# Two changes to a two-layer encoder kernel: some stores issued by ACT, and the last two projection jobs of the second layer taken unit by unit

## The chip, the cores and the metric

The kernel runs on one core of a Trainium2 chip. The time is the device time of one execution in microseconds (us), as the median of several runs. All engines of the core have their own instruction stream: TensorE (PE, with its weight loads shown apart as PEld), VectorE (DVE), ScalarE (ACT), GpSimd (POOL) and SyncE (SP). SP computes nothing here: before the change it issues every DMA of the program.

## The reference

Two groups of tokens go through the same trunk of two layers with the same weights: `x_sample` (1024 tokens, "s" in tile names) and `x_prompt` (512 tokens, "p"). The width is 1024, all in float32. Each layer is

```
h = rmsnorm(x, pre_g) * (1 + scale) + shift        # shift, scale, gate: from c by a matmul
p = h @ w_in                                       # one projection, split into columns
mixed = concat(mixer1(p) * silu(gate1), mixer2(p) * silu(gate2))
x = x + gate * rmsnorm(mixed @ w_out, post_g)
```

Layer 0 mixes with dense attention over 8 query heads that share 2 key heads (mixer A: q and k normalised and rotated), and with a mixture of three dilated sliding windows over 8 heads (mixer B). Layer 1 mixes with attention over a neighbourhood of 8 rows by 16 columns with a learned bias (mixer C, 12 heads), and with a two-dimensional Fourier transform followed by a linear map (mixer D).

## The kernel before

**Units and jobs.** The 1536 tokens are three units of 512: units 0 and 1 are the group s, unit 2 is the group p. A projection is cut into jobs of 256 output columns. In layer 1 the jobs are `u0`, then `k`, `q`, `v` for three blocks of heads (`k0 q0 v0 k1 ...`), and then the gates `g0 g1 g2 d0`. A job loads its weights in four chunks (`load_w`, L375): DMA into a staging tile `ws`, a rounded copy on ACT (tile `wh...`), and the rest of the value on POOL or DVE (`wl...`). A product is then three matmuls: high by high, high by low, low by high. A gate job on one unit is two accumulations of 24 matmuls with 512 columns each (`chan_gemm`; tiles `c1g` for g0 to g2, `c1d` for d0).

**Through memory.** What a projection gives is stored to scratch tensors in HBM and loaded again by the attention. Staging tiles for this are three buffers (tag `sp`, `SPB` = 3). Some are filled by ACT alone: `spill` (L434; tiles `spkb` and `spqb`, k and q of mixer B), and `half_v` (L455; `vstvb`, v of mixer B, and `vst1v`, v of mixer C). The stores to `k0`, `q0`, `vb0` and `v1` follow. Others are filled by ACT and DVE together (`spill_hl`, `spill_gate`).

**The output projection** of a unit needs its operand first (`s3_operand`, L891). For each of eight slices k it loads the mixer's output (`m`) and the gate (`g`) into one of the three `sp` buffers (tile `og`), multiplies them (POOL and DVE in turn, L912), rounds on ACT (`hhm`, L913) and takes the rest on DVE (`hlm`, L914). The products are the tiles `y`, 256 columns a matmul, weights `who` and `wlo`.

**Attention units.** A unit of mixer B is one pair of heads on 512 queries: scores (`sbs`, `sbp`), softmax (DVE, ACT, DVE on the tiles `ebs`, `ebp`), transposes (`pt1bs`, `pt2bs`), copies out of PSUM, and products with v (`obs`, `obp`). In the listings below `obs701` is the product for pair 7 of group s, first half of its queries, second head; `obs410` is pair 4, second half. Mixer C has scores `scs`, transposes `ptcs`, products `ocs` with v tiles `Vcs`.

**The order.** The program names work in the order of `run`. The framework's scheduler (`schedule_with_timeline_sim=True`, L1419) then orders the instructions of each engine by a modelled timeline, so that projection matmuls are put between those of the attention. Each engine runs its list in that order. Every DMA signals on one of eight semaphores, given out in turn, and first waits until the one that had it before has landed. All DMAs are issued at L140.

**The place of the second part.** The end of layer 1's projection goes job by job: in each job unit 0 and then unit 1. In the last job, `d0`, the operand of unit 2's output projection, `s3_operand(1, 2)`, is named between unit 0 and unit 1 (`mid`, L1369). Then follows `s3(1, 2)`, the output projection of unit 2.

Of the kernel before, what the change touches and what calls it, by code (L numbers as in the profile page):

```python
# [122 lines left out]
class Body:  # L123
# [10 lines left out]
        self.read_b = None  # L134


    def dma(self, dst, src):

        dst, src = (t.bitcast(F32) if t.dtype == F32R else t for t in (dst, src))
        self.nc.sync.dma_start(dst, src)  # L140

    def mm(self, out, l, r, start, stop):
        self.nc.tensor.matmul(out, l, r, start=start, stop=stop, skip_group_check=True)  # L143
# [220 lines left out]
    def w_pair(self, shape, name):  # L364
        self.wn += 1
        if self.wend:
            tags, bufs = self.wend[self.wn % len(self.wend)]
            pool = self.wx if tags[0][:2] == "wx" else self.sb
        elif self.wx and self.wn % (WB + WX) >= WB:
            pool, tags, bufs = self.wx, ("wxh", "wxl"), WX  # L370
        else:
            pool, tags, bufs = self.sb, ("wh", "wl"), WB
        return [pool.tile(shape, F32R, tag=t, name=f"w{x}{name}", bufs=bufs) for x, t in zip("hl", tags)]
# [60 lines left out]
    def spill(self, ps, dst, u, scale, nm, classes=False):  # L434

        st = self.sb.tile([P, 2, 512], F32, tag="sp", name="sp" + nm, bufs=SPB)[:, 0]
        self.nc.scalar.mul(st, ps, scale)
        if classes:
            dst, st = (x.rearrange("p (r a) -> p r a", r=4) for x in (dst, st))
            self.dma(dst[:, :, P * u:P * u + P], st)  # L440
        else:
            self.dma(dst[:, u * 512:(u + 1) * 512], st)

    def spill_v(self, ps, nh, dst, nm):

# [99 lines left out]
    def s2_0_unit(self, H, u, w, typ, q, nm):  # L545
        pool = self.l0
        g, gu = self.unit_of[u]
        n = g.name
        if typ in ("ga", "gb"):
            for c in range(2):  # L550
                ps = self.pD(f"g{nm}{c}")
                self.chan_gemm(ps, H, w, c)
                self.flush()
                p = 2 * q + c + (4 if typ == "gb" else 0)
                self.spill_gate(ps, self.gd[0, n, gu, p], f"{nm}{c}")
            return
        toks = []
        for jp in range(2):
            i = 4 * gu + 2 * jp
            ps = self.early.pop((nm, jp), None)  # L560
            if ps is None:
                ps = self.pD(f"t{nm}{jp}").rearrange("p (t c) -> p t c", t=2)
                self.tok_gemm(ps, H, w, jp)
            else:
                self.tok_gemm(ps, H, w, jp, 4)
            if jp == FLUSH:
                self.flush()
            if typ == "vb":
                dst = self.vd[0, n, q].rearrange("(r a) d -> r a d", r=4)[2 * jp:2 * jp + 2, P * gu:P * gu + P]
                self.dma(dst.rearrange("t p d -> p t d"), self.half_v(ps, f"{nm}{jp}"))  # L570
                continue
            js = slice(i, i + 2)
            t = pool.tile([P, 2, 256], F32, tag="qt", name=f"qt{nm}{jp}", bufs=QTB)
            toks.append(t)
            if typ == "kva":
                dst = self.vd[0, n, "a"][i * P:(i + 2) * P].rearrange("(t p) h d -> p t h d", t=2)
                self.spill_v(ps[:, :, 128:256], 2, dst, f"{nm}{jp}")
                self.qk_a(ps[:, :, 0:128], 2, self.tab[:, js], t[:, :, 0:128], f"{nm}{jp}")
            elif typ == "qa":
                self.qk_a(ps, 4, self.tab[:, js], t, f"{nm}{jp}")  # L580
            else:
                self.qk_b(ps, 4, self.tabb[:, js], t, f"{nm}{jp}")
        if typ == "vb":
            return

        def finish():
            for c in range(1 if typ == "kva" else 2):
                pt = (self.pT if self.idle else self.pD)(f"qT{nm}{c}")

                for j in range(4):  # L590
                    o = pt[:, j * P:(j + 1) * P]
                    if typ == "qb":
                        o = pt.rearrange("p (t r a) -> p r t a", t=4, r=4)[:, j]
                    self.tr(o, toks[j // 2][:, j % 2, c * P:(c + 1) * P])
                if typ == "kva":
                    self.spill_hl(pt, self.kd[0, n, 0], gu, 1.0, nm)
                elif typ == "kb":
                    self.spill(pt, self.kd[0, n, 4 + 2 * q + c], gu, 1.0, f"{nm}{c}", g.U > 1)
                elif typ == "qb":
                    self.spill(pt, self.qd[0, n, 4 + 2 * q + c], gu, 0.125, f"{nm}{c}")  # L600
                else:
                    self.spill_hl(pt, self.qd[0, n, 2 * q + c], gu, 0.125, f"{nm}{c}")
        self.late.append(finish)
# [413 lines left out]
        self.Gd = [[dr.tile([P, 2, 256], F32R, name=f"G{x}{cs}") for x in "hl"] for cs in range(2)]  # L1017
        self.bias_dr = dr.tile([16, NCH, 24, 32], F32, name="bias_dr")

    def s2_1_job(self, Hs, us, kind, mid=None):  # L1020
        base = dict(q=0, k=768, v=1536, g=2304, u=3072, d=3328)
        typ, q = kind[0], int(kind[1])
        c0 = base[typ] + 256 * q
        w = self.load_w(self.a["w_in_cd"][0][:, c0:c0 + 256], f"1{kind}{us[0]}", W1)
        for i, u in enumerate(us):
            if i == 1 and mid:
                mid()
            self.s2_1_unit(Hs[u], u, w, typ, q, f"1{kind}{u}")

    def s2_1_unit(self, H, u, w, typ, q, nm):  # L1030
        nc, pool = self.nc, self.sb
# [2 lines left out]
        if typ == "v":  # L1034
            for jp in range(2):
                gr = 2 * gu + jp
                ps = self.pD(f"t{nm}{jp}").rearrange("p (t c) -> p t c", t=2)
                self.tok_gemm(ps, H, w, jp)
                st = self.half_v(ps, f"{nm}{jp}").rearrange("p t (h d) -> p t h d", h=2)
                for t in range(2):  # L1040
                    self.dma(self.vd[1, n, q][:, 2 * t:2 * t + 2, :, gr, :].rearrange("h r c d -> (r c) h d"), st[:, t])
            return
        for c in range(2):
            ps = self.pD(f"c{nm}{c}")
# [205 lines left out]
    def run(self):  # L1250
# [85 lines left out]
        with tc.tile_pool(name="l1", bufs=1) as self.l1:  # L1336
# [26 lines left out]
            for kind, i in zip(jobs[:LEAD], ST2):  # L1363
                step(i[0])
                self.s2_1_job(Hs, [0], kind)
                step(i[1])
            for n, kind in enumerate(jobs):

                mid = (lambda: ops.append(self.s3_operand(1, 2))) if n == len(jobs) - 1 else None  # L1369
                self.s2_1_job(Hs, [1] if kind in jobs[:LEAD] else [0, 1], kind, mid)  # L1370
                if n == 0:
                    second, third = self.fourier(gs)
                if n == FS[0]:
                    four = second()
                if n == FS[1]:
                    third(*four)
                    for q in range(3):
                        self.attn_c(gp, 0, q)
                elif kind[0] == "v":
                    for h in range(2):  # L1380
                        self.attn_c(gs, h, int(kind[1]))
            _, H = self.s3(1, 2, H=ops[0], last=lambda: self.s3_operand(1, 0))
            self.wend = ([(("wh", "wl"), WB)] * WB + [(("wxh", "wxl"), WX)] * WX + [(("qh", "ql"), QB)] * QB +
                         [(("pth", "ptl"), PTB)] * PTB + [(("V", "V"), VB)] * (VB // 2))
# [38 lines left out]
```

## Time and profile before

| | |
|---|---|
| time, median of 3 runs | 1926.3 us (1924.66 to 1928.03) |
| the profiled execution, its own time | 1924.99 us |
| its span, first to last instruction | 1923.1 us |
| PE busy in the span | 1851.2 us, 96% |
| DVE busy | 1204.1 us, 63% |
| ACT busy | 927.0 us, 48% |
| POOL busy | 596.2 us, 31% |
| mean granted clock of PE | 0.986 |

PE is busy nearly all the time, so the reading starts from the 72 us in which it is not, and from the stretches in which its granted clock is 0.5 and not 1. The waits say on whom an engine stood; the timeline of one engine shows single instructions with the idle time before them in square brackets; the windows view gives busy time, granted clock and DMA share of a stretch.

### The profile page before, as it was taken

The page shows a single profiled execution, that of the slowest core. Times are in us where ns is not written, and L with a number is a line of the kernel's source. Part 1 is how long each engine was busy: PE and PEld are TensorE (multiplying, and loading weights), DVE is VectorE, ACT ScalarE, POOL GpSimd, SP SyncE. Part 2 cuts the span into 40 slices and gives each one's busy share as a digit, 9 for nine tenths or more (in the row PEclk, how much of TensorE's full clock was granted, in tenths as well). Part 3 has the DMA queues.
Part 4 walks back from the last instruction along what each step waited for, and adds up shares of the span by engine and source line. Part 5 has one row for each costly group of instructions (what it writes and reads, how often), then busy time and mean ns, then how long its engine had stood idle before and what let it go on. Part 6 is the DMA issues. An engine that isn't in the chain of part 4 may idle for free.

```text
span 1923.1 us, 37887 instructions
## 1 busy us (share of the span) xinstructions
PE 1851.2 (96%) x13752; PEld 1618.0 (84%) x13752; DVE 1204.1 (63%) x3110; ACT 927.0 (48%) x2197; POOL 596.2 (31%) x534
## 2 busy tenths in 40 slices
PE   7999999999999999999999989999999999998998
PEld 5789768999998988889977677888988888887998
DVE  2688863254767666767676687663666666664633
ACT  3456543343356554556554455553544444452421
POOL 3631224354722111121111121443423444322410
PEclk9999999999999999999999999999999999998999
DMA  9754455466663323234345563663777676655743
GB/s 305 252 176 150 125 143 183 124 200 216 230 208 119 104 87 115 69 121 144 118 149 156 163 213 111 219 194 125 224 228 222 201 241 192 205 170 185 234 150 143
DMA packets 255050, 332.51 MB, mean 173 GB/s; under 512 B 25624, under 2 KB 172408, under 8 KB 254864
## 3 DMA queue, kind: packets, MB, share of 16 engines
q1 hardware_dynamic: 254864, 330.10, 54.1%
q8 instruction: 108, 1.77, 0.4%
q14 instruction: 78, 0.64, 0.1%
HBM read 248.42 MB, written 81.61 MB: 172 GB/s over the span
## 4 chain that ended last, share of the span: by engine, by line
PE 41%; DMA 7%; DVE 3%; POOL 1%; issue 1%; ACT 1%; SPq 0%; POOLq 0%; ACTq 0%; DVEq 0%
PE y L143 6%; PE c1g L143 5%; PE c1q L143 5%; PE c1k L143 5%; PE t1v L143 4%; DMA Vcs<-v1s 2%; PE ocs L676 2%; PE ptcs L147 2%; PE scs L143 1%; PE obs L676 1%; PE c1d L143 1%; DMA og<-g1s 1%; PE sbs L807 1%; PE oas L143 1%; DMA og<-g0s 1%
## 5 line engine op out<-in xcount | busy, mean ns | idle before, releaser
L143 PE MATMUL y<-who,hhm 128*128 128x256 f32 x768 | 221.2, 290 | 7.7 <-ACT hhm L913 7.3
L143 PE MATMUL y<-who,hlm 128*128 128x256 f32 x768 | 220.5, 290 | 5.1 <-DVE hlm L914 5.1
L143 PE MATMUL y<-wlo,hhm 128*128 128x256 f32 x768 | 219.5, 288 | 2.5 <-DVE wlo L386 1.4
L143 PEld LDWEIGHTS y<-who,hhm 128*128 128x128 f32 x768 | 149.7, 195 | 11.1 <-ACT hhm L913 9.5
L143 PEld LDWEIGHTS y<-who,hlm 128*128 128x128 f32 x768 | 149.2, 195 | 8.3 <-DVE hlm L914 6.9
L143 PEld LDWEIGHTS y<-wlo,hhm 128*128 128x128 f32 x768 | 149.5, 195 | 4.3 <-DVE wlo L386 1.8
L724 ACT ACTIVATE eas<-sas,nmas 128x512 f32<-128x512 f32 x128 | 87.0, 685 | 71.4 <-DVE nmas L720 71.1
L1105 POOL TENSOR_TENSOR bics<-TTcs,mkc 128x288 f32<-128x288 f32 (+1 forms) x72 | 65.1, 904 | 144.4 <-DVE mcs L1119 118.8
L654 DVE TENSOR_TENSOR ptlas<-ptas,pthas 128x512 fp32r<-128x512 f32 x128 | 85.6, 684 | 19.6 <-ACT pthas L652 18.8
L386 POOL TENSOR_TENSOR wlo<-wso,who 128x512 fp32r<-128x512 f32 x40 | 58.2, 1458 | 116.0 <-ACT who L385 112.9
L715 DVE TENSOR_REDUCE mxas<-sas 128x1 f32<-128x512 f32 x128 | 86.2, 682 | 12.1 <-PE sas L143 11.6
L1124 ACT ACTIVATE ecs<-ecs,ngmcs 128x288 f32<-128x288 f32 (+1 forms) x96 | 55.0, 573 | 66.3 <-DVE ngmcs L1122 62.5
L652 ACT CAST pthas<-ptas 128x512 fp32r<-128x512 f32 x128 | 70.6, 591 | 28.3 <-PE ptas L147 24.9
L143 PE MATMUL t1v<-wh1v,hh 128*128 128x256 f32 x288 | 83.2, 290 | 0.0
L143 PE MATMUL t1v<-wl1v,hh 128*128 128x256 f32 x288 | 83.1, 289 | 0.0
L143 PE MATMUL t1v<-wh1v,hl 128*128 128x256 f32 x288 | 82.2, 286 | 0.0
L936 ACT ACTIVATE ysq<-y 128x256 f32<-128x256 f32 x96 | 36.7, 382 | 88.3 <-PE y L143 65.4
L147 PE MATMUL ptas<-ident,eas 128*128 128x128 f32 x512 | 76.6, 273 | 0.3 <-DVE eas L732 0.3
L385 ACT CAST who<-wso 128x512 fp32r<-128x512 f32 x80 | 48.6, 617 | 48.4 <-PE y L143 10.4
L912 POOL TENSOR_TENSOR og<-og 128x512 f32<-128x512 f32 x24 | 33.9, 1414 | 114.5 <-DMA og<-g0s 32.2
L143 PE MATMUL oas<-pthas,Vas 128*128 128x256 f32 x256 | 68.9, 284 | 0.0
L143 PE MATMUL oas<-ptlas,Vas 128*128 128x256 f32 x256 | 68.5, 294 | 0.2 <-DVE ptlas L654 0.2
(631 smaller groups left out, 6324.4 us busy)
## 6 DMA issues: line engine op xcount, KB each, us to landing
wso<-w_out_ab SPq DMA_DIRECT2D x48, 256.0 KB
kcs<-k1s SPq DMA_DIRECT2D x24, 384.0 KB
wso<-w_out_cd SPq DMA_DIRECT2D x32, 256.0 KB
ws1k<-w_in_cd SPq DMA_DIRECT2D x28, 256.0 KB
wskb<-w_in_ab SPq DMA_DIRECT2D x24, 256.0 KB
wsqb<-w_in_ab SPq DMA_DIRECT2D x24, 256.0 KB
wsvb<-w_in_ab SPq DMA_DIRECT2D x24, 256.0 KB
ws1q<-w_in_cd SPq DMA_DIRECT2D x24, 256.0 KB
```

Of the source, the lines that this page charges most:

```text
L143: self.nc.tensor.matmul(out, l, r, start=start, stop=stop, skip_group_check=True)
L147: self.nc.tensor.transpose(out, in_, self.ident[:k, :k])
L385: nc.scalar.copy(hi, st)
L386: (nc.vector if c in dve else nc.gpsimd).tensor_sub(lo, st, hi)
L652: nc.scalar.copy(h[:rows, :w], pt[:rows, :w])
L654: nc.vector.tensor_sub(lo[:rows, :w], pt[:rows, :w], h[:rows, :w])
L676: return self.nc.tensor.matmul(out[x:x + HD], v, p, start=n < 2, stop=False, tile_position=(0, x), skip_group_check=True)
L715: nc.vector.tensor_reduce(mx[:, c:c + 1], ps, op=ALU.max, axis=AX.X, negate=True)
L724: nc.scalar.activation(e[:, 512 * c:512 * c + 512], pss[c], AF.Exp, bias=nmx, accum_out=den[:, c:c + 1])
L936: nc.scalar.activation(sq[:, 0:256], ps[:, t], AF.Square, accum_out=ss[j][:, job:job + 1])
L1105: nc.gpsimd.tensor_add(b, T[:, :, wo:wo + w], self.mcol[:, kind, wo:wo + w].unsqueeze(1).to_broadcast([P, nrow, w]))
L1124: nc.scalar.activation(e, e, AF.Exp, bias=ngm, scale=0.125, accum_out=den)
```

## The change

Two things are done. First, `dma` takes the engine that issues: `spill`, the stores of `half_v` for `vb0`, and those for `v1` are issued by ACT, 72 DMAs in all (12 each for k and q of mixer B, 12 for its v, 36 for the v of mixer C). They stand in ACT's list behind the instruction that fills the tile, one to seven places later. All other DMAs stay with SP. Second, the last two jobs of layer 1, `g2` and `d0`, go unit by unit: both on unit 0, then `s3_operand(1, 2)` is named, then both on unit 1. Both jobs' weights are kept for that; those of `d0` go to four of the five buffers with the tag `x`. The scheduler orders the whole program anew, so that instructions move in other places too.

```
-    def dma(self, dst, src):
+    def dma(self, dst, src, queue=None):
...
-        self.nc.sync.dma_start(dst, src)
+        (queue or self.nc.sync).dma_start(dst, src)
...
             pool = self.wx if tags[0][:2] == "wx" else self.sb
+            if len(tags) == 1:
+                t = pool.tile([P, 4, 256], F32R, tag=tags[0], name="w" + name, bufs=bufs)
+                return [t[:, 0:2], t[:, 2:4]]
...
-            self.dma(dst[:, :, P * u:P * u + P], st)
+            self.dma(dst[:, :, P * u:P * u + P], st, self.nc.scalar)
         else:
-            self.dma(dst[:, u * 512:(u + 1) * 512], st)
+            self.dma(dst[:, u * 512:(u + 1) * 512], st, self.nc.scalar)
...
-                self.dma(dst.rearrange("t p d -> p t d"), self.half_v(ps, f"{nm}{jp}"))
+                self.dma(dst.rearrange("t p d -> p t d"), self.half_v(ps, f"{nm}{jp}"), self.nc.scalar)
...
+    def w_1(self, kind, u):
         base = dict(q=0, k=768, v=1536, g=2304, u=3072, d=3328)
...
+        c0 = base[kind[0]] + 256 * int(kind[1])
+        return self.load_w(self.a["w_in_cd"][0][:, c0:c0 + 256], f"1{kind}{u}", W1)
...
-                    self.dma(self.vd[1, n, q][:, 2 * t:2 * t + 2, :, gr, :].rearrange("h r c d -> (r c) h d"), st[:, t])
+                    self.dma(self.vd[1, n, q][:, 2 * t:2 * t + 2, :, gr, :].rearrange("h r c d -> (r c) h d"), st[:, t],
+                             self.nc.scalar)
...
-                mid = (lambda: ops.append(self.s3_operand(1, 2))) if n == len(jobs) - 1 else None
-                self.s2_1_job(Hs, [1] if kind in jobs[:LEAD] else [0, 1], kind, mid)
+            for n, kind in enumerate(jobs[:-2]):
+                self.s2_1_job(Hs, [1] if kind in jobs[:LEAD] else [0, 1], kind)
...
+            ws = {}
+            for u in range(2):
+                for kind in jobs[-2:]:
+                    if u == 0:
+                        self.wend = [(("x",), XB)] if kind == jobs[-1] else None
+                        ws[kind] = self.w_1(kind, 0)
+                        self.wend = None
+                    self.s2_1_unit(Hs[u], u, ws[kind], kind[0], int(kind[1]), f"1{kind}{u}")
+                if u == 0:
+                    ops.append(self.s3_operand(1, 2))
```

Three places show how the order moves. SP in layer 0, group p, between the attention of pairs 6 and 7: `kbp70` is the load of pair 7's keys, the `bias_dr` rows store the shifted bias of layer 1, `wsgb` are weights. Before:

```order
L140 DMA m0p5_163<-ofbp501_2881 64x512
L140 DMA bias_dr_216<-rpb_4729 288x1x32 x10
L140 DMA g0p00_150<-gtga020_3960 128x512
L140 DMA bias_dr_216<-rpb_4729 288x1x32
L140 DMA wsgb020_4075<-w_in_ab 128x2x256
L140 DMA bias_dr_216<-rpb_4729 288x1x32
L140 DMA kbp70_3546<-k0p7_146 128x512
```

The same place of SP now:

```order
L140 DMA m0p5_163<-ofbp501_2881 64x512
L140 DMA bias_dr_216<-rpb_4729 288x1x32
L140 DMA kbp70_3546<-k0p7_146 128x512
L140 DMA bias_dr_216<-rpb_4729 288x1x32 x4
L140 DMA g0p00_150<-gtga020_3960 128x512
L140 DMA bias_dr_216<-rpb_4729 288x1x32 x4
L140 DMA wsgb020_4075<-w_in_ab 128x2x256
```

The load of the keys stands behind one store of the bias now, not behind twelve.

PE in layer 0, group s, mixer B, at the product `obs701` and the scores of the next unit (`sbs412`), before:

```order
L676 MATMUL obs701_11915<-ptc1bs7011_11931,V1bs70_11732 64x128
L676 MATMUL obs701_11915<-ptc2bs7010_11941,V2bs700_11738 64x4x32 x2
L676 MATMUL obs701_11915<-ptc2bs7010_11941,V2bs701_11740 64x4x32 x2
L147 MATMUL pt1bs4100_12103<-ident_63,ebs4100_11976 128x128 x2
L143 MATMUL y0000_15152<-who0000_15130,hlm000_15063 128x256
L143 MATMUL y0000_15152<-who0000_15130,hhm000_15062 128x256
L143 MATMUL y0000_15152<-wlo0000_15131,hhm000_15062 128x256
L143 MATMUL y0001_15207<-who0000_15130,hlm000_15063 128x256
```

The same place of PE now:

```order
L679 MATMUL obs701_11915<-ptc1bs7011_11931,V1bs70_11732 64x128
L679 MATMUL obs701_11915<-ptc2bs7010_11941,V2bs700_11738 64x4x32 x2
L679 MATMUL obs701_11915<-ptc2bs7010_11941,V2bs701_11740 64x4x32 x2
L147 MATMUL pt1bs4100_12103<-ident_63,ebs4100_11976 128x128
L810 MATMUL sbs4120_12040<-kbs41_11962,qbs41_11964 128x256
L810 MATMUL sbs4121_12041<-kbs41_11962,qbs41_11964 128x256
L815 MATMUL sbs4120_12040<-kbs41_11962,qbs41_11964 32x256
```

No product of the output projection stands between the attention's matmuls there now. Counted in the whole listing from the first row of `obs501` to the first of `obs411`, PE had 126 projection matmuls of 512 columns and 97 of 256, and now has 10 and 95; the others stand earlier.

SP at the end of layer 1's projection, where the operand of unit 2 is loaded (`og12k`; `g1s` are stores of gates, `m1s` stores of attention), before:

```order
L140 DMA og120_23046<-m1p0_174 128x512
L140 DMA m1s5_131<-ofcs111_22538 64x512
L140 DMA og120_23046<-g1p00_166 128x512
L140 DMA g1s07_117<-gt1d001_23040 128x512
L140 DMA og121_23052<-m1p1_175 128x512
L140 DMA og121_23052<-g1p01_167 128x512
L140 DMA og122_23060<-m1p2_176 128x512
L140 DMA og122_23060<-g1p02_168 128x512
```

The same place of SP now:

```order
L140 DMA m1s4_130<-ofcs91_22312 64x512
L140 DMA og120_22984<-m1p0_174 128x512
L140 DMA og120_22984<-g1p00_166 128x512
L140 DMA og121_22990<-m1p1_175 128x512
L140 DMA og121_22990<-g1p01_167 128x512
L140 DMA g1s07_117<-gt1d001_22978 128x512
L140 DMA og122_22998<-m1p2_176 128x512
L140 DMA og122_22998<-g1p02_168 128x512
```

The operand's loads begin two heads of the attention earlier (behind the store of `ofcs91`, not beside that of `ofcs111`), and both jobs on unit 1 come behind them on PE: 96 matmuls of 512 columns where there were 48.

## Rows read from the trace of the kernel before

**Rows 1.** The page's span, and its first part: busy time of each engine.

```profile
span 1923.1 us, 37887 instructions
PE 1851.2 (96%) x13752; PEld 1618.0 (84%) x13752; DVE 1204.1 (63%) x3110; ACT 927.0 (48%) x2197; POOL 596.2 (31%) x534
```

**Rows 2.** Waits of PE: who for whom, us in total, times, longest.

```profile
PE y L143 <- ACT hhm L913: 7.3, 5, 3.3
PE ocs L676 <- DMA Vcs<-v1s: 6.4, 6, 1.5
```

**Rows 3.** Windows: stretch, length, PE, PEld, DVE, ACT, POOL, clock, DMA share, GB/s.

```profile
1756.60:1760.50 3.90, 0.65 (x4) 0.45 (x4) 3.90 (x4) 1.73 (x3) 3.23 (x2) 1.00 0.43 150
1760.50:1774.20 13.70, 8.97 (x35) 7.86 (x36) 5.77 (x9) 3.02 (x6) 1.51 (x1) 0.50 0.72 239
...
265.50:268.90 3.40, 3.40 (x27) 2.17 (x27) 2.01 (x12) 0.59 (x1) 0.00 (x0) 0.50 0.66 185
1108.60:1115.40 6.80, 6.05 (x40) 4.50 (x40) 6.00 (x16) 3.75 (x8) 1.28 (x1) 0.50 0.61 161
1090.00:1109.00 19.00, 15.89 (x159) 10.45 (x158) 12.27 (x31) 8.83 (x18) 3.38 (x3) 0.99 0.76 235
```

**Rows 4.** Timeline of PE, 1735 to 1790: start, us, instruction, [idle before <-releaser].

```profile
1755.26 0.39 PE L143 MATMUL c1d<-hh,wl1d 128*128 128x512 f32 x1
1755.48 0.28 PE L143 MATMUL y<-who,hhm 128*128 128x256 f32 x1
1755.60 0.28 PE L143 MATMUL y<-wlo,hhm 128*128 128x256 f32 x1
...
1758.79 0.39 PE L143 MATMUL y<-who,hlm 128*128 128x256 f32 x1 [2.20 <-DVE hlm L914]
...
1765.58 0.58 PE L143 MATMUL y<-who,hhm 128*128 128x256 f32 x1 [3.33 <-ACT hhm L913]
```

**Rows 5.** Timeline of SP's issues, 1722 to 1785.

```profile
1739.19 0.37 SPq L140 DMA_DIRECT2D og<-m1p  x1
1744.61 0.45 SPq L140 DMA_DIRECT2D m1s<-ofcs  x1
1745.11 0.58 SPq L140 DMA_DIRECT2D og<-g1p  x1
...
1763.41 0.42 SPq L140 DMA_DIRECT2D og<-g1p  x1
```

**Rows 6.** Timeline of ACT, 1728 to 1780.

```profile
1749.80 0.62 ACT L913 CAST hhm<-og 128x512 fp32r<-128x512 f32 x1 [4.53 <-POOL og L912]
...
1769.39 0.62 ACT L913 CAST hhm<-og 128x512 fp32r<-128x512 f32 x1
```

**Rows 7.** Timeline of SP and then of PE around 250 to 265.

```profile
251.15 7.44 SPq L140 DMA_DIRECT2D bias_dr<-rpb  x10
...
261.55 0.84 SPq L140 DMA_DIRECT2D kbp<-k0p  x1
...
255.09 0.45 PE L812 MATMUL sbp<-kbp,qbp 64*32 64x128 f32 x16
...
264.92 0.49 PE L807 MATMUL sbp<-kbp,qbp 64*128 64x128 f32 x4 [2.39 <-DMA kbp<-k0p]
```

**Rows 8.** Windows of the tile y alone, in the stretch without other projection work.

```profile
1090.00:1109.00 19.00, 3.63 (x22) 2.87 (x22) 0.00 (x0) 0.00 (x0) 0.99 0.76 235
```

**Rows 9.** Instructions on the tile vst1v: the stores' issues on SP, min/median/max ns.

```profile
L140 SPq DMA_DIRECT2D v1s<-vst1v x24: 360/471/1087, 1368.5 to 1630.6; - x24
```

**Rows 10.** Waits of SP behind ACT, and of DVE behind ACT.

```profile
SPq L140 <- ACT vstvb L458: 22.4, 6, 10.3
SPq L140 <- ACT vst1v L458: 16.9, 7, 8.5
DVE rdas L728 <- ACT eas L724: 75.2, 58, 2.4
```

**Rows 11.** Chain of work that ended last: start, us, what.

```profile
1495.01 9.65 DMA Vcs<-v1s
```

More of the change, by code (lines that the diff above doesn't have):

```diff
@@ L1018, in scratch1, with s2_1_job @@
         self.bias_dr = dr.tile([16, NCH, 24, 32], F32, name="bias_dr")
-    def s2_1_job(self, Hs, us, kind, mid=None):
+    def w_1(self, kind, u):
         base = dict(q=0, k=768, v=1536, g=2304, u=3072, d=3328)
[L1022 to L1028, printed above, removed]
+        c0 = base[kind[0]] + 256 * int(kind[1])
+        return self.load_w(self.a["w_in_cd"][0][:, c0:c0 + 256], f"1{kind}{u}", W1)
+    def s2_1_job(self, Hs, us, kind):
+        w = self.w_1(kind, us[0])
+        for u in us:
+            self.s2_1_unit(Hs[u], u, w, kind[0], int(kind[1]), f"1{kind}{u}")
     def s2_1_unit(self, H, u, w, typ, q, nm):
@@ L1366, in run @@
                 step(i[1])
-            for n, kind in enumerate(jobs):
-                mid = (lambda: ops.append(self.s3_operand(1, 2))) if n == len(jobs) - 1 else None
-                self.s2_1_job(Hs, [1] if kind in jobs[:LEAD] else [0, 1], kind, mid)
+            for n, kind in enumerate(jobs[:-2]):
+                self.s2_1_job(Hs, [1] if kind in jobs[:LEAD] else [0, 1], kind)
                 if n == 0:
```

## The prediction

> **What bounds the kernel now.** I read the page's busy times first: PE works for 1851.2 of 1923.1 us, DVE and ACT for far less [rows 1]. An edit that frees SP or ACT is therefore worth something only where PE stands, or where its granted clock is half. So I went to the waits of PE, then to the windows around each wait, and then to the timelines of PE, SP and ACT there.
>
> The largest single wait is that of the output projection's products `y` on ACT's rounding `hhm`, 7.3 us in five places [rows 2]. Most of it is one place, the end of layer 1's projection. The last gate product ends near 1755.5, the products of unit 2 follow, and PE has the operand's first slices only: it works 0.65 us of the 3.9 from 1756.6, and 8.97 of the next 13.7, these at half clock [rows 3]. The timeline shows the two longest stops, 2.20 us on DVE's `hlm` and 3.33 us on ACT's `hhm` [rows 4]. What comes late is the operand itself. SP issues its first load at 1739.19 and its last at 1763.41 [rows 5], ACT rounds the slices from 1749.80 to 1769.39 [rows 6]. That is a chain paced by three staging buffers, begun too late, not a lack of engine time.
>
> The second place is in layer 0: SP issues the load of `kbp70` at 261.55, behind a block of stores of the bias that holds it for 7.44 us and more; PE stands 2.39 us for it at 264.92 [rows 7], and the 3.4 us behind it run at half clock [rows 3].
>
> The third is a stretch without projection work between attention matmuls. From 1090 to 1109 PE works 15.89 of 19.0 us, and from 1108.6 on it has half clock for 6.8 us [rows 3]; only 22 of its matmuls there are products `y` [rows 8].
>
> **Part by part, against the profiled execution's own 1924.99 us.** The median of the three runs lies 1.3 us above it; that is added at the end.
>
> *The last two jobs unit by unit.* Between naming the operand and needing it PE had one job on one unit, 48 matmuls of 512 columns, and now has 96. Their spacing in the timeline is 0.22 us [rows 4], so the cover grows by 48 x 0.22 = 10.6 us. Before, PE passed 1755.48 - 1739.19 = 16.3 us from the first load to the first product [rows 4, 5]; now that is about 27. The operand took from 1739.19 to 1770.0, the end of the last rounding: 30.8 us [rows 5, 6]. In these SP was held from 1739.6 to 1745.1 by one store, `m1s<-ofcs`, issued only at 1744.61 [rows 5]. In the new order that store stands later in the row of loads, so I take 5.5 us off: 25 us needed, 27 there. The stops that can go are 3.9 - 0.65 = 3.25 us and 13.7 - 8.97 = 4.73 us, together 7.98 us; and 8.97 us of work at half clock would take half as long, another 4.5 [rows 3]. That is -12.5 us. What may be left: the store's wait can stand elsewhere among the loads, and then the need is 30.8 again against 27. I take +1.0 us, with 0 and 6 (half of the gain) as ends.
>
> *The load of `kbp70`.* It stands behind one store of the bias now and not behind twelve. Its buffer comes free with the last score of the tile before it, at 255.09 + 0.45 = 255.5. Issued then it would land 3.4 us after its issue, as it did (261.55 to 264.92) [rows 7], so at 259. PE reaches its first reader some 21 matmuls of 512 columns after the tile before it (255.09), at about 261.5 with what else lies between. The wait of 2.39 us goes, and half of 3.4 us of half clock [rows 3, 7]: -4.1 us. If something else ends late there it is 0.
>
> *The stretch in layer 0, mixer B, that loses its projection work.* From `obs501` to `obs411` PE had 126 x 0.22 + 97 x 0.12 = 39.4 us of projection matmuls between those of the attention, and now has 10 x 0.22 + 95 x 0.12 = 13.6 us, by the spacings of 512 and 256 columns [rows 4]. The 25.8 us that moved are not lost: they run earlier, where PE was full. But the attention's chains (scores, softmax, transposes) are then bare. What that costs is shown by the stretch that is bare already: 3.1 us idle in 19.0, in which 22 x 0.12 = 2.6 us are `y` [rows 3, 8], and half clock for 6.05 us of work, 3.0 us [rows 3]. That is 6.1 us for 13.3 us of attention matmuls. The listing shows about one stretch of that size more than before: +6. The low end is 0, if the 95 matmuls of 256 columns still lie where the chains are long; the high end is two such stretches, +12.
>
> *72 stores on ACT.* On SP such an issue takes 0.47 us in the median, from 0.36 to 1.09 [rows 9]. On ACT they are 72 x 0.47 = 34 us on an engine that is busy 48% [rows 1]. Each also waits until the earlier transfer on its semaphore has landed, and until its tile is made, which ACT itself does, one to seven places ahead. Queued behind it are the rounding of weights and the attention's exponentials; for these DVE waits already, 75.2 us in 58 places [rows 10], and behind DVE the transposes on PE. Most of that lies beside projection matmuls: PE's own waits behind ACT are 7.3 us for `hhm` and little else [rows 2]. The ends are 0 and 34 us. I take +2, near the low end, since the rows of PE hardly show ACT.
>
> *What SP gains.* SP stood 22.4 us behind `vstvb` and 16.9 us behind `vst1v` [rows 10], and now goes past these. PE has no wait that ends on the loads behind them, but for the six on `Vcs`, 6.4 us [rows 2]. These stand on a load of 9.65 us [rows 11] into buffers that the preceding head must first set free; SP's place is not what is late. I take 0, ends -6.4 and +2 (a load that now runs beside others).
>
> *The sum:* -12.5 + 1.0 - 4.1 + 6 + 2 = -7.6 us, so 1917.4 for the profiled execution and **1918.7 us** for the median.
>
> **The rivals.** *Nothing is lost* (the bare stretch and ACT's stores cost nothing): 1924.99 - 12.5 + 1.0 - 4.1 + 1.3 = 1910.7. For it speaks that ACT is idle half the time and that 95 matmuls are left; against it the stretch at 1090.
>
> *The bare stretch costs double*, 12 us: 1924.7. For it: a chain that is late makes the next one late on the same engines. Against it: the idle time was 3.1 us in 19.0, not half.
>
> *The operand is still late* by half of the gain, +6 in place of +1: 1923.7. For it: SP is in order, and a store of attention data still stands among the operand's loads. Against it: the cover grows by 10.6 us, more than the 7.98 us of stops.
>
> *ACT's stores show on PE*, the case that ends slower. A store holds ACT at its semaphore and through its issue; exponentials and roundings behind it come late, DVE after them, and PE has no other work in the bare stretches. If half of each issue, 0.22 us, reached PE, the cost is 72 x 0.22 = 15.8 us in place of 2, and the time 1932.5. It is slower than the bound below from (1930.2 - 1918.7 + 2) / 72 = 0.19 us a store. For it speaks DVE's 75.2 us behind ACT [rows 10], against it PE's short list of waits [rows 2]. [...]
>
> That the change doesn't do what it says is possible for its first part: a store on ACT still waits for the earlier transfer of its semaphore and may leave no sooner than from SP. Since no gain is booked for it, this alone leaves the sum as it is.
>
> **How the numbers follow.** Forecast 0.45 (1914 to 1922 by itself), nothing lost 0.20, bare stretch double 0.14, operand late 0.09, ACT's stores 0.12. A difference under 0.2%, 1922.4 to 1930.2, is about what a measurement of this kernel can't tell from no change. The first two cases are faster, 0.65; the next two within, 0.23; the last slower, 0.12. The range goes from 1908, where the `Vcs` waits are gone too in part, to 1928, past both cases of no change; it leaves out the slower one and the low end.
>
> **What the profile after would show.** Step one is right if PE has no idle time beyond 2 us between the last `c1d` and the products of unit 2, at full clock; wrong if `hhm` still ends a wait of PE there. Step two is right if PE has no wait on `kbp`. Step three is right if idle time and half clock from `obs501` to `obs411` add up to about 6 us more. Step four is right if waits of PE that end on ACT's tiles in attention grow by no more than 2 us, and wrong if DVE's waits behind `eas` and `ebs` grow by tens and PE's with them. The forecast falls as a whole if the new order opens stretches that I didn't compare, since every engine's row was ordered anew.

## The result, and the profile after

The changed kernel is slower. Its median is 1937.57 us (18 runs, 1927.86 to 1942.53) against 1922.74 us of the kernel before (18 runs, 1918.21 to 1931.48); the ratio is 1.0066, with a 95% interval of 1.0053 to 1.0078. That is some 13 us more (the two medians by themselves lie 14.8 us apart), where 7.6 us less was forecast; the time lies outside the range, on the other side of no change.

The first profile of the changed kernel, at 1927.86 us, is the shortest of its 18 runs. It was therefore profiled once more (`e4_changed_again` below, 1936.25 us, near the median), and where one of the two has to stand for the kernel it is that one. The spans of both, the first profile first:

```profile
span 1926.1 us, 37796 instructions
```

```profile
span 1934.4 us, 37796 instructions
PE 1851.0 (96%) x13752; PEld 1615.8 (84%) x13752; DVE 1189.6 (61%) x3110; ACT 927.8 (48%) x2197; POOL 588.2 (30%) x534
```

Beside [rows 1], PE works as long as before (1851.0 us against 1851.2), and the span is 11 us longer: the loss is time in which PE stands. The waits of PE in the second profile (who for whom, us in total, times, longest) say where, beside [rows 2]:

```profile
PE ocs L679 <- DMA Vcs<-v1s: 8.0, 6, 2.8
PE sbs L810 <- DMA kbs<-k0s: 7.0, 3, 4.7
PE sbs L810 <- issue: 5.7, 1, 5.7
PE y L143 <- ACT hhm L916: 3.1, 3, 1.6
```

The wait on `hhm` has fallen from 7.3 to 3.1 us, as forecast. The two rows of `sbs`, the scores of mixer B, are 12.7 us together. Of these the kernel before has one only, and it is small:

```profile
PE sbs L807 <- DMA kbs<-k0s: 1.9, 2, 1.6
```

Windows at the same times in both kernels (columns as in [rows 3]) show the balance. The kernel before:

```profile
250.00:300.00 50.00, 47.61 (x341) 35.87 (x339) 26.44 (x112) 22.36 (x51) 15.35 (x12) 0.97 0.41 111
1050.00:1100.00 50.00, 49.04 (x381) 34.98 (x379) 31.05 (x80) 23.79 (x51) 7.70 (x6) 1.00 0.56 176
1100.00:1150.00 50.00, 45.94 (x431) 36.49 (x432) 40.23 (x105) 25.86 (x62) 10.76 (x8) 0.93 0.71 221
...
1750.00:1800.00 50.00, 41.80 (x284) 39.07 (x283) 32.82 (x42) 21.50 (x50) 19.86 (x13) 0.86 0.74 239
1800.00:1850.00 50.00, 45.64 (x360) 44.63 (x360) 27.27 (x45) 18.32 (x50) 18.55 (x15) 0.97 0.71 236
```

The changed kernel, second profile:

```profile
250.00:300.00 50.00, 50.00 (x350) 38.64 (x349) 23.05 (x87) 21.62 (x47) 15.46 (x12) 1.00 0.45 121
1050.00:1100.00 50.00, 43.05 (x377) 30.94 (x376) 33.28 (x89) 23.04 (x48) 6.38 (x5) 0.90 0.51 160
1100.00:1150.00 50.00, 38.22 (x370) 25.78 (x370) 34.32 (x96) 23.00 (x54) 6.82 (x5) 0.86 0.45 144
...
1750.00:1800.00 50.00, 46.77 (x323) 41.10 (x322) 31.18 (x52) 21.49 (x47) 15.15 (x11) 1.00 0.74 234
1800.00:1850.00 50.00, 47.45 (x391) 46.74 (x391) 26.93 (x43) 18.81 (x52) 20.52 (x16) 1.00 0.70 239
```

From 1750 to 1850, the place of the second part, PE stood 12.6 us before and 5.8 now, at full clock throughout: the forecast gain is there. From 250 to 300 the wait for `kbp70` is gone. But from 1050 to 1150, the bare stretch, PE stands 6.95 + 11.78 = 18.7 us where it stood 0.96 + 4.06 = 5.0, and the granted clock is 0.90 and 0.86 for 1.00 and 0.93.

At the same times the two kernels don't do quite the same work there, since the changed one has the moved projection products behind it already. So here is the stretch by its ends, from the first matmul of `obs501` to the first of `obs411` (the 85th and the 253rd on the tile `obs`), in the kernel before and then in the changed kernel, second profile:

```profile
1040.29:1132.32 92.03, 88.00 (x737) 64.02 (x736) 62.80 (x160) 46.23 (x98) 18.20 (x14) 0.96 0.59 184
1062.55:1147.16 84.61, 65.87 (x621) 45.51 (x620) 57.59 (x155) 39.19 (x86) 11.55 (x9) 0.86 0.50 160
```

Before, PE stands 4.0 us in it, and half clock takes about 3.5 (an estimate: the busy time by what is missing from a clock of 1; it is somewhat high, since the products `y` of the kernel before stand 0.21 us apart at clock 0.50, from 1769.3 to 1773.8, and 0.12 at 1.00, from 1774.3): 7.5 us lost. Now it stands 18.7 us and half clock takes about 9.2: 27.9 us lost, 20 more. That is more than the whole loss of the kernel. The timeline of PE there (columns as in [rows 4]) has the two long stops:

```profile
1069.82 0.66 PE L815 MATMUL sbs<-kbs,qbs 64*32 64x256 f32 x16
1077.48 1.23 PE L810 MATMUL sbs<-kbs,qbs 64*128 64x128 f32 x8 [5.72 <-issue]
...
1101.11 0.66 PE L815 MATMUL sbs<-kbs,qbs 64*32 64x256 f32 x16
1108.01 1.23 PE L810 MATMUL sbs<-kbs,qbs 64*128 64x256 f32 x4 [4.72 <-DMA kbs<-k0s]
```

And SP's issues of the keys in the same stretch:

```profile
1071.37 0.54 SPq L140 DMA_DIRECT2D kbs<-k0s  x1
...
1103.53 0.32 SPq L140 DMA_DIRECT2D kbs<-k0s  x1
```

There is one key buffer (`KB` = 1). So the keys of the next unit are asked for only when the last scores of the unit before have read it: scores from 1101.11, the load at 1103.53, PE again at 1108.01. Such a round takes about 7 us (6.9 here, 7.7 from 1069.82), and projection products lay over it before. Of the first stop the trace names no releaser ("issue"); that it is the keys' load too is read from its place in the same chain, and not shown.

### The profile page after: what moved, and what is told of

Its sections match the earlier page's. It is cut to its first block, busy times and chain, and to the rows that moved or that the text cites. A ratio compares the mean times of both kernels' runs of the same rounds, so it can differ in the third digit from the quotient of the medians.

```text
span 1926.1 us, 37796 instructions
## 1 busy us (share of the span) xinstructions
PE 1847.4 (96%) x13752; PEld 1612.1 (84%) x13752; DVE 1189.3 (62%) x3110; ACT 928.0 (48%) x2197; POOL 589.9 (31%) x534
## 5 line engine op out<-in xcount | busy, mean ns | idle before, releaser
L388 ACT CAST who<-wso 128x512 fp32r<-128x512 f32 x80 | 48.7, 617 | 50.2 <-PE y L143 12.7
```

The costliest lines, as they stand in the source:

```text
L388: nc.scalar.copy(hi, st)
```

## Experiments

Theory 1, formed on the first profile: the loss is the new order of PE, which leaves mixer B bare; that ACT issues the stores costs nothing by itself. Theory 3, the rival: the stores cost by holding ACT. Theory 2 is about the second part alone. The experiments are called e1 to e12. Each ratio is to executions of the kernel before that were taken along with the experiment; their medians lie between 1922.1 and 1924.5 us, so between experiments the ratios are the better measure.

**The second part alone (e1).** All stores stay with SP.

```
-        (queue or self.nc.sync).dma_start(dst, src)
+        self.nc.sync.dma_start(dst, src)
```

> The second part alone: g2 and d0 unit by unit, all stores issued by SP as before. PE's row keeps its projection matmuls between obs501 and obs411 (126 of 512 and 97 of 256 columns, as in the kernel before), and the load of kbp70 stays behind the bias stores. Theory 1 (the loss of the changed kernel lies in the bare stretch of mixer B): the gain of the operand's cover shows alone, -12.5 + 1 us, so 8 to 14 us less than before, and PE's wait on hhm near the end of layer 1's projection is under 2 us. Theory 2 (the cover is worth little, because the operand is late again): within 4 us of before.

Median 1920.37 us, ratio to the kernel before 0.9981 (0.9966 to 0.9997), so 0.6 to 6.5 us less. The sign is right; the size is under half of theory 1's 8 to 14. Up to head 10 of layer 1, first half, its PE row is that of the kernel before, word for word, so what the second part changes lies behind that.

**The first part alone (e2).** The changed kernel's stores, and the end of layer 1's projection as before.

```
-            for n, kind in enumerate(jobs[:-2]):
-                self.s2_1_job(Hs, [1] if kind in jobs[:LEAD] else [0, 1], kind)
+            for n, kind in enumerate(jobs):
...
+                mid = (lambda: ops.append(self.s3_operand(1, 2))) if n == len(jobs) - 1 else None
+                self.s2_1_job(Hs, [1] if kind in jobs[:LEAD] else [0, 1], kind, mid)
...
```

> The first part alone: the 72 stores issued by ACT, the last two jobs job by job as before. The order of PE is bare from obs501 to obs411 (10 matmuls of 512 and 95 of 256 columns), and kbp70 is early, as in the changed kernel. Theory 1 (bare stretch): slower than the changed kernel by what the second part gains, 8 to 12 us, so 20 to 27 us more than before. If the second part gains nothing: the same as the changed kernel, 12 to 15 us more than before.

Median 1937.45 us, ratio 1.0079 (1.0057 to 1.0101). The whole loss is the first part's. Beside the changed kernel there is no difference that can be told, so the second part is worth little there also.

**Eight of the 72 stores back to SP (e3).** Which stores go to ACT decides the scheduler's order; moving those of `vb0` of group s alone brings projection products back into the stretch.

```
-                self.dma(dst.rearrange("t p d -> p t d"), self.half_v(ps, f"{nm}{jp}"), self.nc.scalar)
+                self.dma(dst.rearrange("t p d -> p t d"), self.half_v(ps, f"{nm}{jp}"), self.nc.scalar if n == "p" else None)
```

> The changed kernel, but the 8 stores of vb0 of group s are issued by SP; the other 64 stay with ACT. This alone gives PE its projection matmuls back between obs501 and obs411 (106 of 512 and 114 of 256 columns, for 10 and 95), and kbp70 stays early. Theory 1 (the order of PE in that stretch costs, ACT's issue does not): 12 to 18 us less than before, with no wait of PE on kbs over 2 us around obs601. Theory 3 (ACT's stores themselves cost, by holding ACT): 64 of 72 stores keep eight ninths of the loss, so 8 to 12 us more than before.

Median 1925.0 us, ratio 1.0021 (1.0002 to 1.0039). With 64 stores still on ACT, two thirds of the loss are gone, which is against theory 3; but it is not the gain that theory 1 asked for.

**The changed kernel again (e4)**, unaltered.

> The changed kernel once more, on the chip of the three others and with a second profile. Its first profile lies 10 us under the median of its runs. Theory 1: 12 to 15 us more than before in the median, and a profile nearer to the median shows more idle time and half clock in the same stretch, 1060 to 1150; if the 10 us lie elsewhere the stretch is as in the first profile within 2 us, and another one grows.

Median 1936.14 us, ratio 1.0072 (1.0048 to 1.0096). Its profile is the one shown above. The stretch from 1060 to 1150 is as in the first profile, so it is not what the two differ by; the 10 us between them lie in no one place.

**The term of the keys in layer 0 (e5).** The second part alone, with the bias stores named later.

```
-                    self.bias_shift()
                     self.s3(0, 2, "e", H)
...
+                if g is gs:
+                    self.bias_shift()
                 for kind in jobs:
```

> The second part alone, and the 16 stores of the shifted bias named later in the program (behind the first jobs of group s), so that SP issues the load of kbp70 before all of them; PE's row is that of the second part alone but for 132 of 11467 rows that change places around them. It measures the term of kbp70 by itself. By the step of the prediction: 4 to 5.5 us less than the second part alone, so 6 to 9 us less than before, with no wait of PE on kbp over 0.5 us near 265. By the other end of that step (something else is late there): within 2 us of the second part alone.

Median 1921.97 us, ratio 0.9988 (0.9970 to 1.0005): the wait on `kbp` is gone and nothing can be measured for it.

**The kernel before again (e6)**, unaltered, for a second profile.

> The kernel before, profiled once more, to see how much of the half clock and of the stops near the end of layer 1's projection is the same in every execution. If the 13.7 us at half clock behind 1760 belong to the kernel, they stand again within 3 us, and the second part's 12.5 us were there to be had. If they were this one execution's, under 8 us at half clock stand there now, and the term of the prediction was read from too dear a row.

One run, 1926.55 us. The end of layer 1's projection has half clock for as long (a mean of 0.86 from 1750 to 1800 in both profiles) and stops of that size again (PE idle for 9.24 us in that window, 8.20 in the first profile); its windows, beside those of the first profile above:

```profile
1750.00:1800.00 50.00, 40.76 (x276) 37.80 (x275) 33.38 (x41) 20.50 (x49) 19.67 (x13) 0.86 0.72 233
1800.00:1850.00 50.00, 45.90 (x360) 44.68 (x359) 26.95 (x44) 18.30 (x52) 18.53 (x15) 0.95 0.72 243
```

So the 12.5 us of the prediction were there in both profiled executions, and what the second part alone gains at its place must be given back elsewhere.

**The 36 stores of layer 1 alone on ACT (e7)**, with the second part. `spill` and the `vb0` stores go back to SP.

```
-            self.dma(dst[:, :, P * u:P * u + P], st, self.nc.scalar)
+            self.dma(dst[:, :, P * u:P * u + P], st)
...
-            self.dma(dst[:, u * 512:(u + 1) * 512], st, self.nc.scalar)
+            self.dma(dst[:, u * 512:(u + 1) * 512], st)
...
-                self.dma(dst.rearrange("t p d -> p t d"), self.half_v(ps, f"{nm}{jp}"), self.nc.scalar)
+                self.dma(dst.rearrange("t p d -> p t d"), self.half_v(ps, f"{nm}{jp}"))
```

> The second part, and of the first part only the 36 stores of v1 (layer 1) issued by ACT; the 36 of layer 0 stay with SP. The order is that of the second part alone up to the first store of v1 in layer 1, and the stretch from obs501 to obs411 keeps 85 matmuls of 512 and 137 of 256 columns. Theory 1 (the order costs, ACT's issue does not): within 3 us of the second part alone. Theory 3 (a store on ACT costs PE 0.2 us or more): 7 us or more above the second part alone.

Median 1935.57 us, ratio 1.0058 (1.0036 to 1.0080). By the expectations this is theory 3's result. But its order changes too from the first store of `v1` on, and two of the stretches that are worse are these; the kernel with the second part alone first, this one behind it (it is some 12 us later there, so its windows hold not quite the same work):

```profile
1200.00:1250.00 50.00, 44.72 (x381) 40.94 (x380) 31.25 (x68) 25.43 (x68) 18.73 (x20) 0.97 0.64 210
1600.00:1650.00 50.00, 48.60 (x389) 43.20 (x388) 32.91 (x111) 24.34 (x64) 19.75 (x22) 1.00 0.62 190
```

```profile
1200.00:1250.00 50.00, 41.83 (x374) 34.60 (x373) 32.44 (x80) 25.07 (x64) 14.45 (x17) 0.93 0.58 195
1600.00:1650.00 50.00, 44.58 (x329) 39.95 (x328) 29.97 (x98) 20.48 (x54) 17.27 (x18) 0.90 0.58 176
```

The first of the two lies at the end of layer 0, where no store of `v1` is issued at all, and is 2.9 us emptier. That points to the order here also. To part the two for good, the order has to be held.

**Order and queue parted.** Both kernels trace the same instructions under the same names, and 72 of them differ in their engine. So each can be given the other's rows: a table of names by engine, and between neighbours a dependency without a wait.

```
+ORDER = {
...
+def pin(tc):
+    have = {i.name: i for i in tc.nc.cur_bb.bb.instructions}
+    for table in ORDER.values():
...
+        for a, b in zip(row, row[1:]):
+            tc.add_manual_dep(have[b], a, mybir.DependencyInfo(mybir.DependencyClass.NoSync, mybir.DependencyReason.DATA),
+                              reason="order")
...
         trunk_kernel(tc, aps, outs)
+        pin(tc)
```

Stores on ACT, order of the second part alone (e8):

> The changed kernel, its 72 stores issued by ACT, but every engine's row pinned (by dependencies without a wait) to that of the second part alone: all instructions of PE, DVE, ACT, POOL and SP other than these stores stand word for word as there. It takes the new order away and leaves the stores on ACT. Theory 1 (the order costs, not the issue on ACT): within 3 us of the second part alone, 1 to 6 us less than before. Theory 3 (the stores on ACT cost): 8 us or more above before.

Stores on SP, order of the changed kernel (e9):

> The other way round: the second part with all stores issued by SP, but every engine's row pinned to that of the changed kernel, but for the 72 stores. It keeps the new order and takes the stores from ACT. Theory 1 (order): as the changed kernel, 10 to 16 us more than before, with the keys' waits in 1060 to 1150. Theory 3 (stores on ACT): as the second part alone, 1 to 6 us less than before.

The first has a median of 1920.41 us, ratio 0.9975 (0.9955 to 0.9995); the second 1937.46 us, ratio 1.0068 (1.0045 to 1.0090). Each goes with its order and neither with its queue: 72 stores on ACT cost and give nothing that can be measured (1920.41 beside 1920.37 us of the second part alone, 1937.46 beside 1937.57 of the changed kernel; the intervals of each pair leave some 5 us either way). In the traces, PE, DVE, ACT and POOL of e8 take their instructions in the order of e1 throughout, and those of e9 in the order of the changed kernel, four matmuls of `ocs` apart. Theory 3 falls. The stretch from `obs501` to `obs411`, first with the stores on ACT and the old order, then with the stores on SP and the new one:

```profile
1038.42:1131.77 93.35, 86.77 (x738) 63.54 (x737) 61.94 (x160) 46.19 (x98) 18.62 (x14) 0.98 0.58 182
```

```profile
1064.39:1149.31 84.92, 65.49 (x622) 45.17 (x621) 57.93 (x155) 39.10 (x86) 11.63 (x9) 0.86 0.50 159
```

Read as above, e8 loses 6.6 + 1.7 = 8.3 us in it, and e9 19.4 + 9.2 = 28.6.

**The keys first, order held (e10).** The load of `kbp70` goes ahead of the bias stores in SP's row of the table, past fourteen DMAs, and nothing else moves.

```
 L140 DMA m0p5_163<-ofbp501_2881 64x512
+L140 DMA kbp70_3546<-k0p7_146 128x512
 L140 DMA bias_dr_216<-rpb_4729 288x1x32 x10
...
-L140 DMA kbp70_3546<-k0p7_146 128x512
```

> The kernel of e8 (stores on ACT, every row pinned to the order of the second part alone) with one load moved: SP issues kbp70 ahead of the bias stores, 6 places earlier; nothing else changes place. It measures the term of kbp70 with the order held. By the step of the prediction: 4 to 5.5 us less than e8, so 7 to 10 us less than before, and no wait of PE on kbp near 265. If the wait is only handed on (the bias stores and the weights behind them come later by the same time): within 2 us of e8.

Median 1919.25 us, ratio 0.9962 (0.9944 to 0.9979); 1.2 us less than e8 by the medians and 2.5 by the ratios, both within what the two intervals leave open. The wait that goes is this one of e8,

```profile
264.00 0.49 PE L810 MATMUL sbp<-kbp,qbp 64*128 64x128 f32 x4 [2.96 <-DMA kbp<-k0p]
```

and the profiled execution with the keys first has none there, but is no shorter (1920.83 against 1919.28 us). It is the fastest kernel of this study by its ratio, and beats both kernels of the case; what sets it above e8 is not measured clearly.

**The weights of d0 later (e11).** In e1 a new stop had come up behind 1680. SP's issues there, with PE's waits, in the second part alone:

```profile
1669.82 0.92 SPq L140 DMA_DIRECT2D ws1d<-w_in_cd  x2
...
1678.04 2.78 SPq L140 DMA_DIRECT2D Vcs<-v1s  x4
```

```profile
1687.38 0.65 PE L679 MATMUL ocs<-ptccs,Vcs 128*64 128x128 f32 x6 [2.26 <-DMA Vcs<-v1s]
1689.48 1.12 PE L679 MATMUL ocs<-ptccs,Vcs 96*64 96x128 f32 x6 [1.45 <-DMA Vcs<-v1s]
```

In the kernel before (second profile) the same loads of `Vcs` are issued at 1671.88, and PE doesn't wait:

```profile
1671.88 2.64 SPq L140 DMA_DIRECT2D Vcs<-v1s  x4
```

The last two weight loads of `d0` come earlier now; SP stands behind them, and the values of the heads come 6 us later. The edit of e11 to SP's row of e10:

```
-L140 DMA ws1d002_22914<-w_in_cd 128x2x256
-L140 DMA ws1d003_22919<-w_in_cd 128x2x256
...
-L140 DMA wso1200_23164<-w_out_cd 128x2x256
-L140 DMA wso1201_23170<-w_out_cd 128x2x256
...
 L140 DMA Vcs810_22098<-v1s2_196 96x1x384
+L140 DMA ws1d002_22914<-w_in_cd 128x2x256
+L140 DMA ws1d003_22919<-w_in_cd 128x2x256
+L140 DMA wso1200_23164<-w_out_cd 128x2x256
+L140 DMA wso1201_23170<-w_out_cd 128x2x256
```

> The kernel of e10 with four more loads moved on SP: the last two weight loads of d0 (ws1d) and the first two of the output projection of unit 2 (wso) come behind the loads of Vcs of heads 10 and 8, not ahead of them; the roundings of these weights are placed anew, the rest stays. In e1 and e8 SP stood some 5 us behind these weight loads near 1665 to 1672, and PE then 1.5 to 3.7 us for Vcs near 1689, partly at half clock. Theory (this is where part of the second part's gain went): 2 to 5 us less than e10, and no wait of PE on Vcs over 0.5 us in 1680 to 1695. Rival (Vcs waits for its buffers, not for SP's place): within 1.5 us of e10.

Median 1919.03 us, ratio 0.9975 (0.9962 to 0.9988): no gain. The stops on `Vcs` shrink to 0.67 us, and another takes their place:

```profile
1681.60 0.65 PE L679 MATMUL ocs<-ptccs,Vcs 96*64 96x128 f32 x6 [0.67 <-DMA Vcs<-v1s]
1686.82 0.61 PE L143 MATMUL scs<-kcs,qhcs 128*128 128x288 f32 x1 [4.09 <-DVE mcs L1123]
```

The last weights of `d0` pass through DVE as well, and by the listing of its row they now stand among the heads' softmax. The wait is handed on from SP to DVE, so SP's place alone was not the cause.

**The bare stretch alone (e12).** From the kernel of e8, the 126 matmuls of 512 columns are taken out of the stretch and put ahead of `obs501`.

```
+L143 MATMUL c1g120<-hh123,wh1g123 128x512
...
 L679 MATMUL obs501<-ptc1bs5010,V1bs50 64x128
```

> The kernel of e8 (stores on ACT, rows pinned to the order of the second part alone) with one thing moved: the 126 projection matmuls of 512 columns that PE has between obs501 and obs411 (products of g1, g2 and d0 on unit 2) stand in one piece ahead of obs501, as the scheduler of the changed kernel puts nearly all of them; their weights, gates and stores are placed anew around them, all else stays. It makes the bare stretch without any of the other changes of order. Theory 1 (the bare stretch is most of the loss): 9 to 16 us more than e8, so 5 to 12 us more than before, with PE's waits on kbs and half clock in 1060 to 1150 as in the changed kernel. The price in the prediction for it: 6 us more than e8. Rival (the loss of the changed kernel is spread over its whole order): under 4 us more than e8.

Median 1939.74 us, ratio 1.0082 (1.0067 to 1.0097), 19 us above e8 by the medians and 21 by the ratios, more than the 9 to 16 of theory 1. One move makes all of the loss and some more. The stretch, in a profile that is the longest of its runs (1946.63 us), and two of the waits of the whole run:

```profile
1068.60:1150.56 81.96, 64.39 (x611) 43.92 (x610) 55.71 (x147) 37.55 (x81) 12.89 (x10) 0.88 0.57 178
```

```profile
PE sbs L810 <- issue: 5.1, 2, 4.1
...
PE sbs L810 <- DMA kbs<-k0s: 3.6, 2, 1.9
```

PE stands 17.6 us in it and half clock takes about 7.7, 25.3 us in all beside 8.3 in e8. So 17 us of the difference lie in the stretch itself.

## Why the prediction was wrong, step by step

*The operand of unit 2* was read rightly at its place and wrongly in the sum. The stops went from 12.6 to 5.8 us and the half clock is gone, 10 us or so of the 11.5. But the second part alone gains 0.6 to 6.5 us, and in the presence of the first part nothing that can be told. The step asked what is late next among the operand's loads; it did not ask what the weights of `d0`, brought forward, would pass on SP and DVE. The price lies in mixer C of group s, just ahead. From the 129th matmul on its scores `scs` to the last product `ocs`, in order the kernel before, the first part alone (e2), the second part alone (e1) and the changed kernel (second profile):

```profile
1638.03:1742.96 104.93, 104.93 (x684) 86.50 (x682) 66.57 (x205) 46.32 (x114) 31.07 (x32) 1.00 0.57 180
1660.22:1765.05 104.83, 104.83 (x684) 86.49 (x683) 68.01 (x207) 47.10 (x115) 31.79 (x33) 1.00 0.57 178
1638.57:1750.33 111.76, 107.70 (x686) 88.12 (x683) 71.43 (x211) 49.38 (x120) 36.77 (x36) 0.98 0.61 188
1659.84:1770.85 111.01, 106.79 (x685) 87.57 (x683) 74.38 (x213) 50.92 (x122) 37.72 (x37) 0.98 0.62 190
```

Where the two jobs go job by job PE never stands there. Where they go unit by unit it stands 4.1 and 4.2 us, and as many matmuls take 6.8 and 6.2 us longer. From there to the last `y` of unit 2 it is 73.64 us before and 64.71 in the second part alone, 65.25 in e2 and 59.09 in the changed kernel: 8.9 and 6.2 us gained. So most of the gain, or all of it, is paid in advance. That e11 only changed the releaser suggests that the price is that of the work itself at that place, not of one queue; this is argued, and which of its parts sets it stays open.

*The load of `kbp70`*: the wait went, as forecast. 4.1 us were booked; the time shows 1.2 to 2.5 us (e10 less e8) or nothing (e5 less e1), each open by some 5 us. At the last score of mixer B of group p the profiled execution of e10 is 4.9 us ahead of that of e8, at the first score of mixer C of group s 3.8, and at its last product 0.3 behind. So the gain was there at its place; how much of it lasts in most executions stays open.

*The bare stretch* is the step that failed. +6 us were booked, with ends 0 and +12; alone it costs 17 to 21 us (e12 beside e8: in the stretch, by the medians, by the ratios), and the kernels of e8 and e9, whose orders differ in most of the program, are 17 us apart. The mechanism was the one named: attention's chains without cover. Its price was not, and first of all the size. The step took one more stretch like that of [rows 3, 8], with 13.3 us of attention matmuls. From `obs501` to `obs411` the kernel before works 88.0 us (its row stands with the result), of which 39.4 are projection products and about 3.5 the price of half clock. That leaves some 45 us of attention matmuls, and 32 of them had been covered. At the step's own rate, 6.1 us for 13.3, these 32 cost 15 us; that is an estimate, and it is 9 more than was booked.

The rate was too low as well. It was taken from [rows 3, 8], the one bare stretch of the kernel before, and this held stops of attention's chain (1.66, 0.73 and 0.29 us) and one of 0.48 us on `hhm`; the keys' load was covered there. A stretch that spans more units than one shows the round of the single key buffer on top, 5.72 and 4.72 us of stops in the changed kernel, and PE has half clock three times around it (13.7, 6.8 and 6.8 us from 1071.3, 1105.5 and 1129.3 in the first profile, where the stops are 5.83 and 5.41 us; the second has a mean clock of 0.90 from 1050 to 1100 and 0.86 from 1100 to 1150) instead of once (6.8 us from 1108.6). The prediction had counted the projection products in the stretch (39.4 against 13.6 us), but not the attention matmuls between them, and could have asked for each load inside it what lay over it. A high end of twice the one stretch was no bound, since no row showed a unit's loads without cover. With 17 to 20 us for this step, 3.6 gained for the operand (e1), 1.2 to 2.5 for the keys and nothing for ACT the sum is 11 to 15 us more, where 13 was measured.

*ACT's stores*: +2 us with ends 0 and 34; e8 beside e1 shows 0, to some 5 us, and this holds what SP gains as well. That was nearly right. The issues on ACT took 0.33 (queries of group p) to 0.53 us (keys of group s) in the median, and DVE's wait on ACT behind the exponentials did not grow (75.2 us in [rows 10]). The first profile:

```profile
L140 ACTq DMA_DIRECT2D v1s<-vst1v x24: 366/367/532, 1381.6 to 1638.5; - x24
L140 ACTq DMA_DIRECT2D k0s<-spkb x8: 521/532/593, 331.6 to 615.9; - x8
L140 ACTq DMA_DIRECT2D q0s<-spqb x8: 338/338/339, 342.7 to 639.0; - x8
```

```profile
DVE rdas L731 <- ACT eas L727: 71.9, 58, 2.6
```

So the rival that ended slower had the sign and not the cause: ACT's stores themselves cost nothing that can be measured. The stores of `v1` for group s took no longer from ACT than from SP (0.37 us in the median beside 0.47 in [rows 9]); eight of the 24 ran beside an issue of SP, and these took 0.37 to 0.48 us.

*What SP gains*: 0 was booked. It was not measured apart from what ACT's stores cost; the two together came to 0.

*The rivals*: the one that named the true mechanism, the bare stretch at double price, stopped at 12 us and so at no change. None of the rivals put the slower side on the order, though the prediction's own last sentence did: "The forecast falls as a whole if the new order opens stretches that I didn't compare". Most of the loss came in one that it had compared. e7 shows that it can be more than one stretch: its order keeps most of the projection work in mixer B and still loses 0.58%, part of it at the end of layer 0 and near 1600. What makes those places worse was not tested by itself.

## What to carry to other kernels

Where a scheduler orders the program, an edit that costs nothing in itself can cost more than it was to gain by the order that it sets off: look for the stretch that lost its filling work, price it by all the work that it holds, and go through the loads inside it one by one, since what a buffer's round trip costs (about 7 us here) is not seen in rows where it was covered. To part an edit from its order, pin the rows of the other version by dependencies without a wait; here that settled in two runs what five with edits of the source had not. And a gain read at its place is only a gain if the work that was brought forward has a place of its own.

## What was not expected of the hardware

That DMAs may be issued from ACT at no cost that can be measured, in a kernel whose ACT is busy for 48%, was not expected: 72 stores, 0.33 to 0.53 us each in the median, and the time is the same within the intervals. The round of one key buffer, from the last score that reads it to the first that reads its new content, is about 7 us (1069.82 to 1077.48, where the trace names no releaser, and 1101.11 to 1108.01), of which 4.5 to 6.1 us lie behind the issue of the load.
